# S5 in five steps per block beside ten gate columns, and six gate columns as three Strassen pairs

## The chip, the cores and the metric

The kernel runs on one core of a Trainium2 chip. The core has a matmul engine (PE), a vector engine (DVE), an activation engine (ACT), a general engine (POOL) and SP, whose queue issues most of the transfers between the chip's memory and the core's SBUF. Each engine works through its own list in order and waits for the others by semaphores. The metric is the device time of one execution in microseconds (us), the median of several.

## The reference, cut to what matters

A decoder layer on 1024 tokens of width 1024 in float32, with a state space branch (S5) and a recurrent branch (LRU) merged by sigmoid gates:

```python
h = rms_norm(x, g_pre)
proj = h @ w_in                       # 1024 x 5632
s5_x, s5_g, lru_x, lru_g, gate_s, gate_l = jnp.split(proj, IN_SPLITS, axis=-1)
y_s = s5_ssm(s5_x, ...)               # 32 groups of 16 channels, 64 complex states
glu_a, glu_b = jnp.split(jax.nn.gelu(y_s) @ w_glu, 2, axis=-1)
z_s = (glu_a * jax.nn.sigmoid(glu_b) * jax.nn.silu(s5_g)) @ w_bs
c = causal_depthwise_conv(lru_x, conv_w, conv_b)
z_l = (rg_lru(c, ...) * jax.nn.silu(lru_g)) @ w_bl
merged = jax.nn.sigmoid(gate_s) * z_s + jax.nn.sigmoid(gate_l) * z_l
x = x + rms_norm(merged @ w_out, g_post)
x = x + (p @ w_ple) * jax.nn.sigmoid(x @ w_ple_gate)
```

`w_in` has 44 columns of 128: 0 to 3 are s5_x, 4 to 7 s5_g, 8 to 27 the LRU's two inputs, 28 to 35 gate_s, 36 to 43 gate_l.

## The kernel before, in words

Every product is made to float32 accuracy from three passes: an operand is split into a high part, which ACT copies out in the reduced format fp32r, and a low part, the rest, which DVE subtracts (L234). `three` (L317, L319) issues high x high, high x low and low x high into one PSUM tile of 128 x 512; this is the wide matmul of the profile. Activations stand with features on partitions, so that a column of a weight matrix costs 8 blocks x 2 halves of the tokens x 3 = 48 wide matmuls.

`weight_plan` writes out the order of all weights: chunks of eight 128 x 128 blocks, loaded by SP into four buffers (`wraw`), and "quads" of four blocks, which become high and low in a ring of six (`wq`). `W.ahead` makes the next quads; a plain quad is used as it is. For some later matrices the kernel uses a Strassen scheme: quads named O2, S1, S3, S4 and A22 are sums of blocks (made on POOL, L194), and seven products stand for eight.

S5 runs in the background. `rows` multiplies one column and calls `tick` after every 12 wide matmuls; a tick advances each generator of the list `bg` to its next `yield`, so that the program's text sets the order on every engine, and S5's instructions fall between the wide matmuls. `s5_params` computes the parameters: DVE and ACT make sine and cosine (L608 to L613), POOL the powers `pw`, the factors `zr` and `zi` (L618 to L654) and the matrix `bb` (L681 to L683). Then DVE multiplies powers and factors into `pzt` (L669 to L675), PE transposes it (`pwT`, L691), and it goes to DRAM as `pt_d` and comes back as `wn`. `s5_ladders` builds the tables of rotations `etab` on DVE (L847 to L856).

For each of eight blocks `s5_main` has seven steps: `wn` is multiplied (L913, L915); py of the block before (8 matmuls, L983 and L984) with its gelu (L986) and four stores to `y_d` (L988), and the loads of the next block (`s5_load`); pkt (L928), which ACT copies to kt and SP writes into the block Toeplitz matrix `toep` in eight transfers (L934); pin (L939); ACT's copies pq (L946), DVE's rotation q, and POOL's weights `ca` for the next block (L902 to L904); four scans (L960) and the rotation back; q put together (L971, L972). py reads toep, ca and q; pin reads wn.

Under S5 lie the columns 36 to 43, 28 to 35, 4 and 5, in that order, each made by `light`: a column into a wide PSUM tile (`ps_L`), a sigmoid on ACT (L1015) into a tile `sg`, for columns 4 and 5 a product on DVE (L1017), and a store to DRAM (L1019). Then the pools of S5 are closed, and the LRU begins.

Of the kernel before, what the change touches and what calls it, by code (L numbers as in the profile page):

```python
# [31 lines left out]
SPAR = (("a_re", 48), ("a_im", 48), ("log_dt", 48), ("d_skip", 32), ("b", 1024), ("c", 1024))  # L32

F_ROWS = (0, 1, 4, 2, 5, 3, 6, 7)


def weight_plan():
    blocks, quads = [], []
# [75 lines left out]
    return blocks, quads  # L114


BLOCKS, QUADS = weight_plan()


FIRST = ("O2",)  # L120
# [15 lines left out]
class Weights:  # L136
# [42 lines left out]
    def sum(self, upto):  # L179
        G = self.nc.gpsimd  # L180
        while len(self.ready) <= min(upto, len(QUADS) - 1):
            i = len(self.ready)
            self.fetch(i)
            q = QUADS[i]
            s = self.sums
            if q[0] == "O2" and len(self.done) < i:
                return

            def add(name, a, b, op, into=None):
                if into is None:  # L190
                    s[name] = self.tmp.tile([P, HT], F32, tag=name, name=f"w{name}_{i}")
                else:
                    s[name] = s[into]
                G.tensor_tensor(s[name], s[a], s[b], op)  # L194

            if q[0] == "plain":
                _, c, o, n = q
# [7 lines left out]
                add("S1", "A21", "A22", ALU.add)  # L205
                add("S2", "S1", "A11", ALU.subtract)
            if q[0] in ("S4", "O4"):
                add("S4", "A12", "S2", ALU.subtract, "S2")
# [4 lines left out]
    def make(self, upto):  # L213
        nc = self.nc
        while len(self.done) <= min(upto, len(QUADS) - 1):
# [37 lines left out]
def tile_hybrid_trunk(  # L253
# [30 lines left out]
    u_d = dram.tile([NS, 8, 16, 8, P], F32, name="u_d")  # L284
    y_d = dram.tile([NS, 8, 8, 16, P], F32, name="y_d")
    pt_d = dram.tile([2, 8, 32 * P], F32, name="pt_d")

    def cst(shape, name, value=None, dt=F32):
        t = const.tile(shape, dt, name=name)
# [397 lines left out]
    def turn():  # L687
        pzt = turned[1]
        ps = px.tile([P, HT], F32, tag="px", name="pwT")
        for n in range(4):  # L690
# [3 lines left out]
        nc.sync.dma_start(pt_d.rearrange("r (h q) (g n) -> (q g) (r h) n", h=2, n=P),  # L694
                          pzs.rearrange("p (m n) -> p m n", n=P))

    prep = s5_params()
    def prep_all(n):
        for i, _ in enumerate(prep):
            if i % n == n - 1:  # L700
                yield

# [30 lines left out]
    def h_lo(k):  # L733
        for h in range(2):
            hi, lo = hplain(k, h)
            (G if h and k else V).tensor_tensor(lo, xt(k, HALF[h]), hi.bitcast(F32), ALU.subtract)  # L736

    def h_pages(names):
        for n, i0 in names:
# [94 lines left out]
    cosv = cosp[:, 32:].rearrange("p (m i) -> p m i", m=8)  # L834
    sinv = sinp[:, 32:].rearrange("p (m i) -> p m i", m=8)
    s5 = {}

    e_tab = {}

    def s5_ladders():  # L840
        t = page(6, "etab", F32)
        e1 = t[:, :512].rearrange("p (r i n) -> p r i n", r=2, i=16)
        e2 = t[:, 512:768].rearrange("p (r i n) -> p r i n", r=2, i=16)
        tm = t[:, 768:1024].rearrange("p (r i n) -> p r i n", r=2, i=16)
        e_tab[1], e_tab[2] = e1, e2
        for e, m0, steps in ((e1, 1, 4), (e2, 5, 3)):
            V.memset(e[:, 0, :, 0:1], 1.0)  # L847
            V.memset(e[:, 1, :, 0:1], 0.0)
            for m in range(steps):
                n = 1 << m  # L850
                er, ei = (v[:, m0 + m, :].unsqueeze(1).unsqueeze(3).to_broadcast([P, 2, 16, n]) for v in (cosv, sinv))
                src, dst, t_ = e[:, :, :, 0:n], e[:, :, :, n:2 * n], tm[:, :, :, :n]
                V.tensor_tensor(dst, src, er, ALU.mult)
                V.tensor_tensor(t_, src, ei, ALU.mult)
                V.tensor_tensor(dst[:, 0], dst[:, 0], t_[:, 1], ALU.subtract)
                V.tensor_tensor(dst[:, 1], dst[:, 1], t_[:, 0], ALU.add)  # L856
                if m % 2:
# [48 lines left out]
    def s5_main(hb, table, before):  # L906
# [11 lines left out]
            dd, ident[:16, :16].unsqueeze(1).to_broadcast([16, 4, 16]),  # L918
            d_skip[:, 4 * hb:4 * hb + 4].unsqueeze(2).to_broadcast([16, 4, 16]), ALU.mult)
        yield  # L920
        before()
        s5_load(hb + 1)
        yield

        kt = wk.tile([P, 576], F32, tag="kt", name=f"kt{hb}")[:16, :HT].rearrange("p (g m) -> p g m", g=4)
        ps = px.tile([P, HT], F32, tag="px", name=f"pkt{hb}")
        for g in range(4):
            T.matmul(ps[32 * g:32 * g + 16, :P], bb_1[:, 4 * hb + g, :],  # L928
                     ca[:, g, 0:8, :].rearrange("p d c -> p (d c)"), start=True, stop=True, tile_position=(0, 32 * g))
        for g in range(4):  # L930
            S.activation(kt[:, g, :], ps[32 * g:32 * g + 16, :P], AF.Copy)
        V.tensor_tensor(kt[:, :, 0:16], kt[:, :, 0:16], dd, ALU.add)
        for j in range(8):
            nc.sync.dma_start(toep[j::8, :, 16 * j:P], kt[:, :, 0:P - 16 * j])  # L934
        yield

        pin = px.tile([P, 2, 2, P], F32, tag="px", name=f"pin{hb}")
        for g in range(4):
            T.matmul(pin[:, g // 2, g % 2, :], win[:, g, :], U[:, g, :], start=True, stop=True)  # L939
        next(table, None)  # L940
        yield

# [47 lines left out]
        return finish  # L990

    def s5_all():
        for _ in prep:
            yield
        for _ in range(3):
            yield
        yield from s5_ladders()
        turned[0]()
        yield
        yield  # L1000
        turn()
        yield
        s5_load(0)
        yield from s5_table(0)
        s5_out_weights(0)
        before = lambda: None
        for hb in range(8):
            before = yield from s5_main(hb, s5_table(hb + 1) if hb < 7 else iter(()), before)
        yield
        before()  # L1010
# [11 lines left out]
    def ev_tile(name):  # L1022
        return ev.tile([P, NT], F32, tag="c", name=name)

    u3 = rows(hplain, "u3")
# [7 lines left out]
    bg.append(u_last())  # L1033
    bg.append(s5_all())
    for m in range(ND):
        light(36 + m, sgl_d[m], False, ev_tile)
    for m in range(ND):
        light(28 + m, sgs_d[m], False, ev_tile)
    for m in range(2):
        light(4 + m, sil_d[m], True, ev_tile)  # L1040
    drain()
    s5x.close()

    lctx = ExitStack()
    l1 = lctx.enter_context(tc.tile_pool(name="l1", bufs=1))
# [652 lines left out]
```

## Time and profile before

| | before |
|---|---|
| median of 3 runs | 928.75 us (928.25 to 928.76) |
| the profiled execution's own time | 928.25 us |
| its span | 926.5 us |
| PE busy | 919.0 us, 4228 matmul records |
| DVE, ACT, POOL busy | 624.6, 469.1, 150.6 us |
| moved by DMA | 134.21 MB |

The span runs from the first to the last instruction of the profiled execution; the execution's own time has a little around it. In a row of the timeline the first number is the start in us from the span's start, the second the duration (for a row with xN, of the N together), then engine, line, operation, output and inputs, shape, and in brackets how long the engine stood before it and what released it. Durations of matmuls overlap, so their spacing is read from the starts.

### The profile page before, as it was taken

Reading aid. Unit: us, or ns where it says so; the run is one execution under the profiler, and the core shown is the slowest. Engines: PE = TensorE matmul, PEld = TensorE weight load, DVE = VectorE, ACT = ScalarE, POOL = GpSimd, SP = SyncE. Lnnn points to the kernel's source line nnn. Section 1 sums busy time; section 2 is a strip of 40 time slices with the busy share of each in tenths; the row PEclk is TensorE's granted clock in tenths of the full one; section 3 lists DMA queues with packets and bytes.
Section 4 is the critical chain, followed back from the end, with each engine's and each line's share of the span. In section 5 each row is a group of like instructions: output and inputs, shape, how many; then the busy total and the mean of one; then the engine's idle time right before and its main releaser. Section 6 shows DMA issues by size and latency. Waiting matters only on the chain.

```text
span 926.5 us, 11716 instructions
## 1 busy us (share of the span) xinstructions
PE 919.0 (99%) x4228; PEld 760.3 (82%) x4228; DVE 624.6 (67%) x977; ACT 469.1 (51%) x714; POOL 150.6 (16%) x159
## 2 busy tenths in 40 slices
PE   9999999999999999999999999999999999999997
PEld 7888888888888888888888888888888887887886
DVE  6885566666664347766666767687862798886863
ACT  6643233444443356666666668544534355558531
POOL 1218112212220000000000000022322126422100
PEclk9999999999999999999999999999999999999999
DMA  9745445564533201111111116811479975499951
GB/s 358 277 126 160 126 142 166 172 171 133 173 97 113 74 29 52 52 46 51 52 52 52 47 34 216 291 56 55 141 255 244 247 193 206 119 245 233 301 184 56
DMA packets 70442, 134.21 MB, mean 145 GB/s; under 512 B 18416, under 2 KB 32880, under 8 KB 70384
## 3 DMA queue, kind: packets, MB, share of 16 engines
q1 hardware_dynamic: 64768, 122.72, 41.7%
q0 software_dynamic: 5472, 10.49, 6.3%
q8 instruction: 33, 0.54, 0.2%
q10 hardware_dynamic: 144, 0.26, 0.1%
q14 instruction: 25, 0.20, 0.1%
HBM read 95.30 MB, written 27.53 MB: 133 GB/s over the span
## 4 chain that ended last, share of the span: by engine, by line
PE 89%; issue 6%; DMA 2%; DVE 1%; POOL 1%; ACT 0%; POOLq 0%; SPq 0%
PE ps_L L319 16%; PE ps_L L317 8%; PE ps_rx L319 8%; PE ps_rg L319 8%; PE ps_rg L317 4%; PE ps_rx L317 4%; PE ps_F L319 3%; PE ps_u L319 3%; PE bZ L319 3%; PE ps_pg L319 2%; PE bW L319 2%; PE pg L319 2%; PE bX L319 2%; PE ps_ple L319 2%; PE ps_ea L319 2%
## 5 line engine op out<-in xcount | busy, mean ns | idle before, releaser
L319 PE MATMUL ps_L<-hB,wq 128*128 128x512 f32 x640 | 197.4, 390 | 0.0
L319 PEld LDWEIGHTS ps_L<-hB,wq 128*128 128x128 f32 x640 | 120.3, 188 | 24.3
L317 PE MATMUL ps_L<-hB,wq 128*128 128x512 f32 x320 | 127.1, 397 | 0.0
L222 ACT ACTIVATE wq<-wraw 128x512 fp32r<-128x512 f32 (+1 forms) x188 | 112.5, 613 | 24.1 <-issue 9.2
L234 DVE TENSOR_TENSOR wq<-wraw,wq 128x512 fp32r<-128x512 f32 (+1 forms) x152 | 105.0, 706 | 3.1 <-ACT wq L222 3.1
L319 PE MATMUL ps_rg<-hB,wq 128*128 128x512 f32 x320 | 98.5, 389 | 0.0
L319 PE MATMUL ps_rx<-hB,wq 128*128 128x512 f32 x320 | 98.5, 389 | 0.0
L319 PE MATMUL ps_pg<-x1hl,wq 128*128 128x512 f32 x240 | 74.9, 392 | 0.3 <-DVE x1hl L1374 0.2
L317 PEld LDWEIGHTS ps_L<-hB,wq 128*128 128x128 f32 x320 | 60.2, 188 | 13.3 <-issue 1.7
L319 PEld LDWEIGHTS ps_rg<-hB,wq 128*128 128x128 f32 x320 | 60.1, 188 | 12.5
L319 PEld LDWEIGHTS ps_rx<-hB,wq 128*128 128x128 f32 x320 | 60.1, 188 | 12.4
L194 POOL TENSOR_TENSOR wS<-wraw 128x512 f32<-128x512 f32 x8 | 12.4, 1549 | 354.8 <-DMA wraw<-w_blocks 343.3
L1078 DVE SCALAR_TENSOR_TENSOR c<-ps_rx,cp_t,c 128x1023 f32<-128x1023 f32 (+2 forms) x30 | 38.5, 1282 | 46.2 <-ACT c L1076 45.5
L317 PE MATMUL ps_rx<-hB,wq 128*128 128x512 f32 x160 | 62.3, 389 | 0.0
L317 PE MATMUL ps_rg<-hB,wq 128*128 128x512 f32 x160 | 62.3, 389 | 0.0
L319 PEld LDWEIGHTS ps_pg<-x1hl,wq 128*128 128x128 f32 x240 | 44.8, 188 | 11.5 <-DVE x1hl L1374 1.7
L1015 ACT ACTIVATE sg<-ps_L 128x1024 f32<-128x1024 f32 x20 | 20.5, 1027 | 59.7 <-issue 52.5
L226 POOL DMA_DIRECT2D wq<-wraw x36 | 31.8, 883 | 100.1 <-ACT wq L225 65.6
L317 PE MATMUL ps_pg<-x1hl,wq 128*128 128x512 f32 x120 | 47.0, 391 | 0.0
L319 PE MATMUL ps_u<-hB,wq 128*128 128x512 f32 x128 | 39.8, 392 | 0.4 <-DVE hB L736 0.4
L319 PE MATMUL ps_F<-ys,wq 128*128 128x512 f32 x128 | 39.4, 389 | 0.0
L1086 ACT ACT_TABLE_LOAD x9 | 11.5, 1283 | 51.2 <-DVE yr L1115 51.2
(360 smaller groups left out, 1927.0 us busy)
## 6 DMA issues: line engine op xcount, KB each, us to landing
wraw<-w_blocks SPq DMA_DIRECT2D x95, 512.0 KB
wq<-wraw POOLq DMA_DIRECT2D x36, 256.0 KB, 6.0
xt<-x_t SPq DMA_DIRECT2D x8, 512.0 KB
ple_d<-ple_sb SPq DMA_DIRECT2D x8, 512.0 KB
wn<-sbt SPq DMA_DIRECT2D x8, 512.0 KB
sgl_d<-sg SPq DMA_DIRECT2D x8, 512.0 KB
wn<-pt_d SPq DMA_DIRECT2D x16, 256.0 KB
sgs_d<-sg SPq DMA_DIRECT2D x8, 512.0 KB
```

What stands on the lines that cost most here:

```text
L194: G.tensor_tensor(s[name], s[a], s[b], op)
L222: nc.scalar.activation(hi, src, AF.Copy)
L226: nc.gpsimd.dma_start(lo.bitcast(F32), src, accum_op=ALU.add)
L234: self.nc.vector.tensor_tensor(lo, src, hi.bitcast(F32), ALU.subtract)
L317: T.matmul(ps, wh, xh, start=start, stop=False, skip_group_check=more)
L319: T.matmul(ps, a, b, start=False, stop=stop and a is (wh if xl_last else wl), skip_group_check=more)
L1015: S.activation(t, ps, AF.Sigmoid)
L1078: V.scalar_tensor_tensor(c[:, d:], ps[:, :NT - d], w_[3 - d], c[:, d:], ALU.mult, ALU.add)
L1086: S.activation(sq, ps, AF.Sigmoid)
```

## The change

The order of the weights: columns 4 and 5 come first under S5, then 36 to 43 as before; 28 and 29 stay plain, and 30 to 35 become three pairs. So ten gate columns, 12 with columns 4 and 5, lie beside S5, where 18 and a part of the next stage lay before.

```diff
+PAIRS = (30, 32, 34)
@@ weight_plan
-    for m in (*range(36, 44), *range(28, 36), 4, 5):
+    for m in (4, 5, *range(36, 44), *range(28, PAIRS[0])):
         plain(col("w_in", m, range(ND)))
+    first = [b for ks in (lo, hi) for m in PAIRS for b in col("w_in", m, ks)]
+    for o in range(0, len(first), 8):
+        light.add(chunk(first[o:o + 8]))
+        cut((len(blocks) - len(first[o:o + 8]), len(first[o:o + 8])))
+    for m in PAIRS:
+        c0, c1 = (chunk(col("w_in", m + i, range(ND))) for i in range(2))
+        light.add(c0)
+        quads.extend((part, c0, c1, 4) for part in ("O2", "S1", "S3", "S4", "A22"))
@@ Weights
-                G.tensor_tensor(s[name], s[a], s[b], op)
+                (self.nc.vector if light else G).tensor_tensor(s[name], s[a], s[b], op)
...
-            if q[0] == "plain" and BLOCKS[q[1][0]][0] in self.BY_DMA and i < len(QUADS) - 2 * ND:
+            if q[0] in ("plain", "A22") and (q[1] in LIGHT or BLOCKS[q[1][0]][0] in self.BY_DMA
+                                             and i < len(QUADS) - 2 * ND):
                 nc.scalar.activation(lo, src, AF.Copy, scale=-1.0)
                 nc.gpsimd.dma_start(lo.bitcast(F32), src, accum_op=ALU.add)
```

The light quads' sums are made on DVE, and the lows of the six plain ones and of A22 by ACT and an accumulating transfer of POOL's queue.

S5 starts before the column u3 instead of after it, its ladders run as a generator of their own, and a block has five steps:

```diff
@@ h_lo
+        nc.sync.dma_start(h_d[k], xt(k))
@@ s5_main
         yield
         before()
         s5_load(hb + 1)
-        yield
+        if hb == 7:
+            h_load(2, "T2", "B22")
...
+        pin = px.tile([P, 2, 2, P], F32, tag="px", name=f"pin{hb}")
+        for g in range(4):
+            T.matmul(pin[:, g // 2, g % 2, :], win[:, g, :], U[:, g, :], start=True, stop=True)
         for g in range(4):
             S.activation(kt[:, g, :], ps[32 * g:32 * g + 16, :P], AF.Copy)
...
-        yield
-
-        pin = px.tile([P, 2, 2, P], F32, tag="px", name=f"pin{hb}")
-        for g in range(4):
-            T.matmul(pin[:, g // 2, g % 2, :], win[:, g, :], U[:, g, :], start=True, stop=True)
+        if hb == 7:
+            h_load(6, "T4", "B21")
@@ s5_all
-        for _ in prep:
-            yield
-        for _ in range(3):
-            yield
-        yield from s5_ladders()
+        for at in prep:
+            if at == "trig":
+                bg.append(s5_ladders())
+            yield
...
         for hb in range(8):
+            if hb == 6:
+                bg.append(t_early())
+            if hb in (2, 5):
+                yield
             before = yield from s5_main(hb, s5_table(hb + 1) if hb < 7 else iter(()), before)
@@
+    bg.append(s5_all())
     u3 = rows(hplain, "u3")
...
-    bg.append(s5_all())
+    for m in range(2):
+        light(4 + m, sil_d[m], True, ev_tile)
```

The normalised input h is stored to DRAM (`h_d`, eight stores of 512 KB) and its quarters B11, B12, B21, B22 are read back into free pages (`h_load`, 16 reads of 256 KB); DVE makes of them the operands T1 to T4 of the scheme (`t_early`, `t_build`). After S5 the pools are closed, four pages and single PSUM banks take their place, and the pairs run:

```diff
+    s5x.close()
+    gp = gctx.enter_context(tc.tile_pool(name="gp", bufs=1))
+    page_pool.update({i: gp for i in (14, 15, 16, 17)})
...
+    wide_ctx.close()
+    gps = gctx.enter_context(tc.tile_pool(name="gps", bufs=1, space=PSUM))
+    bg.append(t_build())
+    for p_ in range(3):
+        tick()
+        lprod(xs[p_], hq["B11"], True)
+        S.activation(lu[:, p_], xs[p_], AF.Copy)
+        tick()
+    for p_, m in enumerate(PAIRS):
+        lprod(xs[p_], hq["B21"], False)
+        gate_out(m, 0, o, xs[p_])
...
+    for p_, m in enumerate(PAIRS):
+        lprod(z, lop["T2"], True)
+        V.tensor_tensor(z, z, u, ALU.add)
...
+        lprod(w_, lop["T1"], True)
...
+        lprod(z, lop["T3"], False)
+        lprod(w_, hq["B22"], False)
+        lprod(z, lop["T4"], False)
...
+    pw2 = wide_ctx.enter_context(tc.tile_pool(name="pw2", bufs=3, space=PSUM))
```

`lprod` is 12 wide matmuls, `gate_out` a sigmoid and its store. PE has 36 wide matmuls fewer in all.

The first place is PE around the transposition `pwT`. Before, it stands in the third column under S5 (`ps_L` is a gate column, `hB` the parts of h, `wq` the quads):

```order
L319 MATMUL ps_L_985<-hB_376,wq_821 128x512
L319 MATMUL ps_L_985<-hB_375,wq_821 128x512
L691 MATMUL pwT<-ident,pzt 128x128 x4
L317 MATMUL ps_L_985<-hB_373,wq_821 128x512
L319 MATMUL ps_L_985<-hB_374,wq_821 128x512
```

In the changed kernel the rows at the same place read (the lines of `three` are L329 and L331 there):

```order
L329 MATMUL ps_u_716<-hB_446,wq_545 128x512
L331 MATMUL ps_u_716<-hB_447,wq_545 128x512
L331 MATMUL ps_u_716<-hB_446,wq_545 128x512
L703 MATMUL pwT<-ident,pzt 128x128 x4
L329 MATMUL ps_L_876<-hB_374,wq_549 128x512
L331 MATMUL ps_L_876<-hB_375,wq_549 128x512
```

pwT has moved from row 401 of PE's list to row 293, between the column u3 (`ps_u`) and the first column under S5. On DVE, what stands ahead of it there, from the cosine on:

```order
L625 TENSOR_SCALAR cosp<-scratch 128x160
L656 RECIPROCAL scratch<-scratch 128x32
L681 TENSOR_TENSOR pzt<-pw,scratch 128x256
L683 TENSOR_TENSOR pzt<-pzt 128x256
L684 TENSOR_TENSOR pzt<-pw,scratch 128x256
L686 TENSOR_TENSOR pzt<-pzt 128x256
L687 TENSOR_TENSOR pzt<-pzt,sgn 128x256
L720 MEMSET etab 128x16
L726 TENSOR_TENSOR etab<-etab,cosp 128x32
```

Before, the ladders (`etab`) came ahead of `pzt`; now they come behind it.

The second place is a block's work on PE. Before, 12 wide matmuls stand between py and pkt, and 12 between pkt and pin:

```order
L983 MATMUL py_1471<-U_1112,toep 128x128
L984 MATMUL py_1471<-q_1379,ca_1200 128x128
L317 MATMUL ps_L_1494<-hB_373,wq_1269 128x512
L319 MATMUL ps_L_1494<-hB_375,wq_1269 128x512
L928 MATMUL pkt_1513<-ca_1384,bb 16x128 x4
L317 MATMUL ps_L_1494<-hB_373,wq_1269 128x512
L319 MATMUL ps_L_1494<-hB_375,wq_1269 128x512
L939 MATMUL pin_1543<-U_1305,wn_1301 128x128 x4
L317 MATMUL ps_L_1494<-hB_441,wq_1338 128x512
```

In the changed kernel:

```order
L999 MATMUL py_1155<-U_903,toep 128x128
L1000 MATMUL py_1155<-q_1062,ca_985 128x128
L944 MATMUL pkt_1176<-ca_1067,bb 16x128 x4
L948 MATMUL pin_1181<-U_1012,wn_1008 128x128 x4
L329 MATMUL ps_L_1096<-hB_444,wq_928 128x512
```

py, pkt and pin now stand together, and 60 wide matmuls lie between pin and the next py (72 after the second and the fifth pin).

The third place is the end of S5. On SP, ahead of the last block's toep (`fT` are the quarters of h, `wraw` the weights, `y_d` the output of block 6, `kt` the last pkt):

```order
L1041 DMA sgl_d<-sg_2087 128x1024
L172 DMA wraw_2137<-w_blocks 128x1024
L1087 DMA fT_2168<-h_d 128x512 x3
L172 DMA wraw_2139<-w_blocks 128x1024
L1087 DMA fT_2197<-h_d 128x512 x3
L1004 DMA y_d<-ysb_2153 8x16x128 x4
L953 DMA toep<-kt_2173 16x512
L953 DMA toep<-kt_2173 16x4x112
```

Before, a gate's store, one weight load and the four stores to `y_d` stood there. On ACT, behind the last block's py:

```order
L1002 ACT_TABLE_LOAD
L1002 ACTIVATE ysb_2309<-py_2310 128x512
L1037 ACT_TABLE_LOAD
L1037 ACTIVATE sg_2324<-ps_L_2227 128x1024
L232 ACTIVATE wq_2346<-wraw_1952 128x512
L236 ACTIVATE wq_2346<-wraw_1952 128x512
L1144 ACTIVATE lu<-lX_2338 128x512
```

The gelu (`ysb`) stands ahead of the sigmoid (`sg`) of the last plain column, and the first copy of a pair's product (`lu`, from the bank `lX`) behind both.

More of the change, by code (lines that the diff above doesn't have):

```diff
@@ L34 @@
 F_ROWS = (0, 1, 4, 2, 5, 3, 6, 7)
+PAIRS = (30, 32, 34)
 def weight_plan():
-    blocks, quads = [], []
+    blocks, quads, light = [], [], set()
     def chunk(names):
@@ L113, in weight_plan @@
             cut(c)
-    return blocks, quads
-BLOCKS, QUADS = weight_plan()
+    return blocks, quads, light
+BLOCKS, QUADS, LIGHT = weight_plan()
 FIRST = ("O2",)
@@ L185, in sum @@
             s = self.sums
+            light = q[1] in LIGHT
             if q[0] == "O2" and len(self.done) < i:
@@ L207, in sum @@
             if q[0] in ("S4", "O4"):
-                add("S4", "A12", "S2", ALU.subtract, "S2")
+                add("S4", "A12", "S2", ALU.subtract, "A12" if light else "S2")
             if q[0] == "S3":
@@ L286, in tile_hybrid_trunk @@
     pt_d = dram.tile([2, 8, 32 * P], F32, name="pt_d")
+    h_d = dram.tile([ND, P, NT], F32, name="h_d")
     def cst(shape, name, value=None, dt=F32):
@@ L695, in turn, with s5_ladders @@
                           pzs.rearrange("p (m n) -> p m n", n=P))
+    cosv = cosp[:, 32:].rearrange("p (m i) -> p m i", m=8)
+    sinv = sinp[:, 32:].rearrange("p (m i) -> p m i", m=8)
+    e_tab = {}
+    def s5_ladders():
+        t = page(6, "etab", F32)
+        e1 = t[:, :512].rearrange("p (r i n) -> p r i n", r=2, i=16)
+        e2 = t[:, 512:768].rearrange("p (r i n) -> p r i n", r=2, i=16)
+        tm = t[:, 768:1024].rearrange("p (r i n) -> p r i n", r=2, i=16)
+        e_tab[1], e_tab[2] = e1, e2
+        for e, m0, steps in ((e1, 1, 4), (e2, 5, 3)):
+            V.memset(e[:, 0, :, 0:1], 1.0)
+            V.memset(e[:, 1, :, 0:1], 0.0)
+            for m in range(steps):
+                n = 1 << m
+                er, ei = (v[:, m0 + m, :].unsqueeze(1).unsqueeze(3).to_broadcast([P, 2, 16, n]) for v in (cosv, sinv))
+                src, dst, t_ = e[:, :, :, 0:n], e[:, :, :, n:2 * n], tm[:, :, :, :n]
+                V.tensor_tensor(dst, src, er, ALU.mult)
+                V.tensor_tensor(t_, src, ei, ALU.mult)
+                V.tensor_tensor(dst[:, 0], dst[:, 0], t_[:, 1], ALU.subtract)
+                V.tensor_tensor(dst[:, 1], dst[:, 1], t_[:, 0], ALU.add)
+                if m % 2 and m0 == 1:
+                    yield
     prep = s5_params()
     def prep_all(n):
-        for i, _ in enumerate(prep):
+        for i, at in enumerate(prep):
+            if at == "trig":
+                bg.append(s5_ladders())
             if i % n == n - 1:
@@ L833, in tile_hybrid_trunk @@
     c_1, c_2 = (g32(cc[:, i]) for i in range(2))
-    cosv = cosp[:, 32:].rearrange("p (m i) -> p m i", m=8)
-    sinv = sinp[:, 32:].rearrange("p (m i) -> p m i", m=8)
     s5 = {}
[L838 to L857, printed above, removed]
-                    yield
     def s5_table(hb):
@@ L1031, in u_last, with lpage, t_low, t_high @@
         yield
-    bg.append(u_last())
+    lf = {}
+    lop = {"T2": [3, 14], "T1": [9, 16], "T3": [17, 2], "T4": [7, 8]}
+    def lpage(n, i):
+        lop[n][i] = quarter(page(lop[n][i], f"l{n}{i}"))
+    def t_low(n):
+        for k in range(4):
+            V.tensor_tensor(lop[n][1][:, k, :], lf[n][:, k], lop[n][0][:, k, :].bitcast(F32), ALU.subtract)
+    def t_high(n):
+        lpage(n, 0)
+        for k in range(4):
+            S.activation(lop[n][0][:, k, :], lf[n][:, k], AF.Copy)
+    def t_subs(n, a, b):
+        for k in range(4):
+            V.tensor_tensor(lf[n][:, k], lf[a][:, k], lf[b][:, k], ALU.subtract)
+            if k % 2:
+                yield
@@ L1034, in tile_hybrid_trunk, with t_early, h_load @@
+    def t_early():
+        yield from t_subs("T1", "T1", "T3")
+        while "T2" not in lf:
+            yield
+        yield
+        yield
+        yield from t_subs("T2", "T2", "T1")
+        t_high("T2")
+        t_high("T1")
+    def h_load(i, t, n):
+        lf[t] = quarter(page(i, f"f{t}", F32))
+        for k in range(4):
+            nc.sync.dma_start(lf[t][:, k], h_d[4 * (n[1] == "2") + k][:, HALF[n[2] == "2"]])
     bg.append(s5_all())
+    u3 = rows(hplain, "u3")
+    bg.insert(0, u_last())
@@ L1035, in tile_hybrid_trunk, with t_build @@
+    for m in range(2):
+        light(4 + m, sil_d[m], True, ev_tile)
     for m in range(ND):
         light(36 + m, sgl_d[m], False, ev_tile)
-    for m in range(ND):
+    for m in range(PAIRS[0] - 28):
         light(28 + m, sgs_d[m], False, ev_tile)
-    for m in range(2):
-        light(4 + m, sil_d[m], True, ev_tile)
     drain()
     s5x.close()
+    gctx = ExitStack()
+    gp = gctx.enter_context(tc.tile_pool(name="gp", bufs=1))
+    page_pool.update({i: gp for i in (14, 15, 16, 17)})
+    def t_build():
+        lpage("T2", 1)
+        t_low("T2")
+        yield
+        lpage("T1", 1)
+        t_low("T1")
+        yield
+        yield from t_subs("T3", "T2", "T3")
+        t_high("T3")
+        yield from t_subs("T4", "T4", "T2")
+        lpage("T3", 1)
+        lpage("T4", 0)
+        for k in range(4):
+            S.activation(lop["T4"][0][:, k, :], lf["T4"][:, k], AF.Copy)
+        t_low("T3")
+        yield
+        lpage("T4", 1)
+        t_low("T4")
@@ new lines, in lprod, with gate_out, gbank @@
+    def lprod(ps, op, start):
+        W.ahead()
+        for k, wb in enumerate(W.next()):
+            three(ps, wb, (op[0][:, k, :], op[1][:, k, :]), start and k == 0, k == 3, not start)
+    def gate_out(m, h, t, src):
+        S.activation(t, src, AF.Sigmoid)
+        nc.sync.dma_start(sgs_d[m - 28][:, HALF[h]], t)
+    wide_ctx.close()
+    gps = gctx.enter_context(tc.tile_pool(name="gps", bufs=1, space=PSUM))
+    def gbank(i, name):
+        return gps.tile([P, HT], F32, tag=f"gb{i}", name=name)
@@ L1044, in tile_hybrid_trunk @@
+    drain()
+    gctx.close()
+    pw2 = wide_ctx.enter_context(tc.tile_pool(name="pw2", bufs=3, space=PSUM))
     lctx = ExitStack()
```

25 lines of the change are left out of this document (24 added, 1 removed).

## The prediction

> **What bounds the kernel now.** I read the page's busy table first, then its chain, then PE's waits.
>
> ```profile
> PE 919.0 (99%) x4228; PEld 760.3 (82%) x4228; DVE 624.6 (67%) x977; ACT 469.1 (51%) x714; POOL 150.6 (16%) x159
> ...
> PE 89%; issue 6%; DMA 2%; DVE 1%; POOL 1%; ACT 0%; POOLq 0%; SPq 0%
> ```
>
> PE (the matmul engine) is busy for 919.0 of 926.5 us and carries 89% of the chain. Its waits (engine, tile, releaser: total, times, longest) say the same:
>
> ```profile
> PE warm L500 <- DVE halfpi L291: 1.1, 1, 1.1
> PE ps_ple L317 <- DVE p_hi L526: 0.8, 1, 0.8
> PE ps_u L319 <- DVE hB L736: 0.4, 1, 0.4
> ```
>
> These are the three longest, two of them at the start. So a matmul taken away is worth its full time, and any wait put on PE costs its full time: there is no slack to hide it in. What a wide matmul costs is read from the column u3, 48 of them between these two starts:
>
> ```profile
> 67.12 0.39 PE L317 MATMUL ps_u<-hB,wq 128*128 128x512 f32 x1
> ...
> 78.00 0.39 PE L317 MATMUL ps_L<-hB,wq 128*128 128x512 f32 x1
> ```
>
> 10.88/48 = 0.2267 us each.
>
> **What is saved.** PE issues 36 wide matmuls fewer (each pair of columns as 7 products of 12, not 8): 36 x 0.2267 = 8.2 us. The S5 matmuls stay, but pkt and pin now stand directly behind py:
>
> ```profile
> 226.35 0.38 PE L983 MATMUL py<-U,toep 128*128 128x128 f32 x2
> ...
> 228.05 0.48 PE L317 MATMUL ps_L<-hB,wq 128*128 128x512 f32 x1
> ...
> 230.96 0.41 PE L928 MATMUL pkt<-ca,bb 128*16 128x128 f32 x8
> 231.31 0.50 PE L317 MATMUL ps_L<-hB,wq 128*128 128x512 f32 x1
> ...
> 234.16 1.05 PE L939 MATMUL pin<-U,wn 128*128 128x128 f32 x8
> 234.97 0.48 PE L317 MATMUL ps_L<-hB,wq 128*128 128x512 f32 x1
> ```
>
> py takes 1.70, pkt 0.35, pin 0.81 us. Joining them can save between nothing and 8 x 0.35 = 2.8 us; I take 0.5, since nothing here shows a cost of turning from one kind to the other.
>
> **First wait: pwT.** It moves from PE's row 401 to row 293, straight behind u3, where PE arrives at 78.00. Its input pzt hangs on a chain that is not moved:
>
> ```profile
> 69.35 1.28 ACT L608 ACT_TABLE_LOAD   x1
> ...
> 72.25 0.25 POOL L618 TENSOR_TENSOR pw<-scratch,cosp 128x32 f32<-128x32 f32 x1 [20.90 <-DVE cosp L613]
> ...
> 83.83 0.25 POOL L654 TENSOR_TENSOR scratch<-scratch 128x32 f32<-128x32 f32 x1
> 84.38 1.09 POOL L681 TENSOR_TENSOR bb<-braw,scratch 128x512 f32<-128x512 f32 x1
> ...
> 98.24 0.42 DVE L669 TENSOR_TENSOR pzt<-pw,scratch 128x256 f32<-128x256 f32 x1
> ...
> 100.61 0.43 DVE L675 TENSOR_TENSOR pzt<-pzt,sgn 128x256 f32<-128x256 f32 x1
> 102.49 0.60 PE L691 MATMUL pwT<-ident,pzt 128*128 128x128 f32 x4
> 102.84 0.47 PE L317 MATMUL ps_L<-hB,wq 128*128 128x512 f32 x1
> ```
>
> The sine's table load stands behind the copies of the third u column on ACT in both kernels, so POOL's powers run from 72.25 to 84.08 as before. Seven DVE operations of pzt use the powers; the first can start before POOL ends, the other six (2.5 us, by the rows of 98.24 to 101.04) can not, so pzt is there at 86.6 at best. It is later if they collide with POOL's bb, as the ladders do now:
>
> ```profile
> 83.06 0.07 DVE L847 MEMSET etab<- 128x16 f32 x1
> ...
> 86.05 1.14 DVE L853 TENSOR_TENSOR etab<-etab,cosp 128x128 f32<-128x128 f32 x1
> ...
> 97.44 0.28 DVE L853 TENSOR_TENSOR etab<-etab,cosp 128x128 f32<-128x128 f32 x1
> ```
>
> The same form takes 1.14 beside POOL and 0.28 without it. All six at 1.14 from 84.1 end at 90.9; I take 88.5. PE therefore waits 8.6 to 12.9 us at pwT. More follows: the ladders (15.2 us from 83.06 to pzt) now come behind pzt on DVE and end near 101 (88.5 + 12.5, since POOL's work runs out near 96), then two lows (1.2), six table operations of 0.35, column 4's product with its sigmoid (1.22) and
>
> ```profile
> 247.89 1.22 DVE L913 TENSOR_TENSOR wn<-wn 128x1024 f32<-128x1024 f32 x1
> 249.15 0.69 DVE L915 TENSOR_TENSOR wn<-wn 128x512 f32<-128x512 f32 x1
> ```
>
> make the first wn ready near 107. Without a wait the first pin would be reached at 78.00 + 0.35 + 72 x 0.2267 + 0.35 = 95.0. So PE's delay at this pin, the wait at pwT within it, is **12 us** (8.6 if the ladders hide; 16 if pzt comes at 90.9 and PE also runs slow behind its wait). Matmuls behind a standstill are slow in this trace:
>
> ```profile
> 7.46 0.63 PE L317 MATMUL ps_ple<-p_hi,wq 128*128 128x512 f32 x1
> ...
> 10.42 0.40 PE L319 MATMUL ps_ple<-p_hi,wq 128*128 128x512 f32 x1
> ```
>
> Seven intervals of 0.42. The Trainium skill, "TensorE: Matmul & The Clock Gate", Part 1, has a rule for it: an idle window of about 3.4 us halves the array's clock, and about 3.4 us of work restore it. By it some 8 matmuls after pwT would take 0.2 us more each, an estimate of 1.6 us; no run here shows a standstill in the middle yet. This would fall ahead of the pin, which waits for DVE anyway, and would not change the sum.
>
> **Second: the rhythm of S5.** Between one pin's end and the next lie 60 matmuls, py and pkt (72 at two places, for the extra steps): 60 x 0.2267 + 1.70 + 0.35 = 15.65 us. Before, the next wn was ready 14.9 us after a pin's end (234.97 to 249.84), so the margin is 0.8 us. DVE has to do it in less time:
>
> ```profile
> 150.00:175.00 25.00, 25.00 (x130) 20.72 (x129) 17.69 (x36) 9.85 (x18) 5.26 (x5) 1.00 0.53 161
> ```
>
> (stretch; busy of PE, PEld, DVE, ACT, POOL; clock, DMA share, GB/s.) DVE worked 0.71 of a period of 22.3 us (84 matmuls and 3.2 us), 15.8 us; two lows of 0.6 drop out, 14.6 remain in a period of 16.5. That is 88%, with collisions that lengthen whatever meets POOL. I put 0.7 us on each of the four plain transitions (0 to 1.5) and none on the two with extra steps. The last is worse, because toep's eight transfers for block 7 now stand on SP behind reads of h and a weight load:
>
> ```profile
> wq<-wraw POOLq DMA_DIRECT2D x36, 256.0 KB, 6.0
> ```
>
> (the accumulating transfers, us from issue to landing) and SP's timeline:
>
> ```profile
> 231.45 2.59 SPq L988 DMA_DIRECT2D y_d<-ysb  x4
> 234.14 5.11 SPq L934 DMA_DIRECT2D toep<-kt  x8
> ```
>
> That load (wraw_2139) reuses a buffer which the accumulating DMAs read, landing some 7.5 us after py6 ends; then three reads, y_d 2.6 and toep 5.1 and its landing make 18.7, where py7 comes at 60 x 0.2267 + 0.35 + 0.81 = 14.8. I count 3.7 (0 to 7). Together **6.5 us** (0 to 13).
>
> The eight stores of h (4 MB) go into the stretch
>
> ```profile
> 25.00:50.00 25.00, 24.63 (x122) 20.22 (x122) 22.75 (x44) 17.25 (x30) 9.21 (x7) 1.00 0.67 238
> ```
>
> whose DMA is idle a third of the time, and weights are loaded ahead: nothing, or 3 us if weights come late.
>
> **Third: the way into the pairs.** S5's pools and the wide PSUM pool close first. lX may start only when ACT has released the last wide tile, and ACT has the gelu of block 7 ahead of it:
>
> ```profile
> 295.33 1.28 ACT L986 ACT_TABLE_LOAD   x1 [5.67 <-issue]
> 296.62 0.60 ACT L986 ACTIVATE ysb<-py 128x512 f32<-128x512 f32 x1
> ...
> 302.08 1.03 ACT L1015 ACTIVATE sg<-ps_L 128x1024 f32<-128x1024 f32 x1
> ```
>
> Table, gelu, table, sigmoid: 1.28 + 0.60 + 1.28 + 1.03 plus handing over, 4.5 us, with PE standing. DVE's lows in S5's memory must also wait until the y_d stores and the last gate's store have landed, some 8 us after py7:
>
> ```profile
> 297.25 2.57 SPq L988 DMA_DIRECT2D y_d<-ysb  x4
> ...
> 304.28 1.29 DVE L234 TENSOR_TENSOR wq<-wraw,wq 128x512 fp32r<-128x512 f32 x2
> ```
>
> From there 30 DVE operations of 0.6 us (the pairs' light sums among them, which POOL would have made before) stand up to the low of lW's weights: 8.2 + 18.2 = 26.4, while PE asks for it at 4.5 + 84 x 0.2267 = 23.5, and the next product's operands end about 1.5 later still. I take **8.5 us** (4.5 to 10.5). Opening the wide pool again waits for the last sigmoid: 0.9 (0 to 1).
>
> **Sum.** 926.5 - 8.2 - 0.5 + 12 + 6.5 + 8.5 + 0.9 = 945.7 us of span. The profiled execution took 928.25 for a span of 926.5, 1.75 more, and the median of the runs lies 0.5 above it: **947 us**. Every wait at its lower bound and the whole 2.8 saved gives 926.5 - 8.2 - 2.8 + 8.6 + 4.5 = 928.6, + 1.75, some 930; every one at its upper gives 926.5 - 8.2 + 16 + 13 + 10.5 + 1 + 3 = 961.8 + 1.75, some 963.
>
> **Rivals.** (a) The rhythm holds, and DVE has its ladders ready under the column after pwT: 926.5 - 8.7 + 8.6 + 0.5 + 8 + 0.9 = 935.8, 938 us. For it: 0.8 us of margin, and lows can slip behind. Against: 88% of DVE. (b) The transfers become the bound: the 150 to 175 row has the DMA engines 0.53 busy, times 22.3/16.5 = 0.72, with the reads of h on top; if toep is then late by 2 us in seven blocks, 947 + 14 = 961. Against: 0.72 is not full. (c) The other side: both standstills hide, because PE takes ready wide matmuls ahead of the waiting pwT and lX; then only the saving counts: 926.5 - 8.7 + 1.75, about 920 us. It decides for faster from the point at which all added waits together stay under 8.7 - 1.9 = 6.8 us. Against it (PE's timeline):
>
> ```profile
> 38.66 0.73 PE L319 MATMUL ps_u<-hB,wq 128*128 128x512 f32 x2 [0.37 <-DVE hB L736]
> 39.23 0.39 PE L317 MATMUL ps_u<-hB,wq 128*128 128x512 f32 x1
> ```
>
> PE stood for 0.37 us ahead of an L319, which reads the low part of h, and started the L317 behind it, which reads the high part that ACT makes first, only afterwards. The Trainium skill, "TensorE: Matmul & The Clock Gate", Part 2, states that matmuls stay in program order and that only weight loads are pulled ahead; the row agrees, and by that rule (c) could not happen.
>
> **Chances.** The forecast 0.68, (a) 0.20, (b) 0.08, (c) 0.04. The range 937 to 958 takes in (a) and most of the upper bounds. A measurement of this kernel tells changes above 0.2% (1.9 us) from none: slower 0.92, within 0.2% of it 0.04 (all lower bounds at once), faster 0.04.
>
> **What would show it.** Right: a wait of PE at pwT on DVE pzt of 8.6 to 12.9 us; a second at the first pin on wn; a third at lX on ACT's sigmoid near 4.5 us and at lW or lZ on lows; waits under 1.5 us at pins two to seven. Wrong: pwT's wait under 5 us, which would mean that POOL's powers start earlier; no wait at lX; or waits at py on toep in every block, which is (b).

## The result and the profile after

The changed kernel took 953.57 us (median of 4 runs, 952.65 to 954.77) beside 928.50 us for the kernel before on the same chip: 1.0271 times the time, 95% interval 1.0253 to 1.0289. It is slower, by 25 us. The forecast was 947, the range 937 to 958.

The page's busy table of the changed kernel (span 952.4 us; the profiled execution took 954.15 us):

```profile
PE 917.3 (96%) x4192; PEld 757.3 (80%) x4192; DVE 658.4 (69%) x1030; ACT 493.0 (52%) x763; POOL 155.0 (16%) x168
...
PE 58%; issue 7%; DVE 6%; DMA 4%; POOL 1%; ACT 1%; SPq 0%; POOLq 0%; DVEq 0%; ACTq 0%
```

The 36 matmuls are gone from PE (4228 to 4192 records). The shares of the chain that ended last can't be set beside those of before: here they add up to 77% only, because the chain as printed reaches back no further than 200.95 us. PE's waits name the places (engine, tile, line, releaser: total, times, longest):

```profile
PE pin L948 <- ACT ysb L1002: 10.4, 7, 1.7
PE pwT L703 <- DVE pzt L683: 6.2, 1, 6.2
PE lX L329 <- ACT sg L1037: 4.3, 1, 4.3
PE pwT L703 <- DVE etab L721: 4.3, 1, 4.3
PE lZ L329 <- ACT lu L1159: 1.2, 1, 1.2
...
PE ps_rx L329 <- ACT lc L1129: 0.7, 1, 0.7
```

Before, the three longest were 1.1, 0.8 and 0.4 us. Nearly all of the loss lies ahead of the first matmul of the LRU, `ps_rx`. It stood here before and stands there now:

```profile
300.55 0.39 PE L317 MATMUL ps_rx<-hB,wq 128*128 128x512 f32 x1
```

```profile
325.87 0.50 PE L329 MATMUL ps_rx<-hB,wq 128*128 128x512 f32 x1 [0.69 <-ACT lc L1129]
```

That is 25.3 us later; from there to the end it is 626.0 us before and 626.5 now. The wait at pwT comes in two pieces, because pzt's four blocks are transposed one by one, and what follows it runs slowly:

```profile
84.12 0.69 PE L703 MATMUL pwT<-ident,pzt 128*128 128x128 f32 x2 [6.19 <-DVE pzt L683]
89.09 0.69 PE L703 MATMUL pwT<-ident,pzt 128*128 128x128 f32 x2 [4.28 <-DVE etab L721]
89.43 0.78 PE L329 MATMUL ps_L<-hB,wq 128*128 128x512 f32 x1
...
94.62 0.40 PE L329 MATMUL ps_L<-hB,wq 128*128 128x512 f32 x1
```

(The second wait is put down to the first row of the ladders; the last operation of pzt, which it really needs, ran directly ahead of that, from 87.89 to 89.03.) Twelve wide matmuls lie between 89.43 and 94.62: 5.19 us where 12 x 0.2267 = 2.72 would do. The same happens behind the wait at lX. Two rows of the stretches (busy of PE, PEld, DVE, ACT, POOL; clock; DMA share; GB/s) show it in the granted clock:

```profile
84.00:95.00 11.00, 6.60 (x18) 5.06 (x19) 10.80 (x16) 4.71 (x6) 10.05 (x9) 0.52 0.45 133
...
143.00:201.00 58.00, 52.98 (x287) 44.28 (x287) 42.19 (x80) 25.27 (x45) 13.62 (x12) 1.00 0.57 162
```

So the account of the waits up to `ps_rx` is: 8.2 saved; 10.5 at pwT and 2.5 for slow matmuls behind it; 10.4 at the seven later pins; 4.3 at lX and 2.3 behind it (12 matmuls from 263.85 to 268.88 in 5.03 us); 1.2 at lZ, 0.7 at ps_rx. That sums to +23.7 of the 25.3. The waits are counted from the end of the matmul before, as the profile models it; read from start to start against the spacings of the kernel before, the same places give 11.1 at pwT and 2.4 behind it, 10.9 at the pins, 4.4 at lX and 2.3 behind it, 1.7 at lZ and 0.8 at ps_rx. With 8.2 saved, and 0.1 saved by joining py, pkt and pin, that is all of the 25.3 us.

The prediction had small waits at the pins, from DVE's load; what causes these was in no step of it. Six of the seven are 1.67 us long. This is one of them, on PE:

```profile
145.17 0.41 PE L944 MATMUL pkt<-ca,bb 128*16 128x128 f32 x8
147.25 0.49 PE L948 MATMUL pin<-U,wn 128*128 128x128 f32 x2 [1.67 <-ACT ysb L1002]
```

ACT in the same stretch:

```profile
145.31 1.28 ACT L1002 ACT_TABLE_LOAD   x1 [2.99 <-issue]
146.60 0.60 ACT L1002 ACTIVATE ysb<-py 128x512 f32<-128x512 f32 x1
```

py, pkt and pin take turns in the PSUM pool `px`, which has two banks. py has one and pkt the other, so pin must wait until the gelu has read py, and the gelu stands behind a table load: 1.28 + 0.60 behind py, 1.67 of it in PE's way.

### The profile page after: what moved, and what is told of

The parts are those of the page before. It is cut to its first block, busy times and chain, and to the rows that moved or that the text cites. A ratio compares the mean times of both kernels' runs of the same rounds, so it can differ in the third digit from the quotient of the medians.

```text
span 952.4 us, 11842 instructions
## 1 busy us (share of the span) xinstructions
PE 917.3 (96%) x4192; PEld 757.3 (80%) x4192; DVE 658.4 (69%) x1030; ACT 493.0 (52%) x763; POOL 155.0 (16%) x168
## 4 chain that ended last, share of the span: by engine, by line
PE 58%; issue 7%; DVE 6%; DMA 4%; POOL 1%; ACT 1%; SPq 0%; POOLq 0%; DVEq 0%; ACTq 0%
PE ps_rx L331 8%; PE ps_rg L331 8%; PE ps_rx L329 4%; PE ps_rg L329 4%; PE bZ L331 3%; PE ps_pg L331 2%; PE ps_L L331 2%; PE bW L331 2%; PE bX L331 2%; PE pg L331 2%; PE ps_F L331 2%; PE lZ L331 2%; PE ps_ea L331 2%; PE ps_eb L331 2%; PE bZ L329 1%
## 5 line engine op out<-in xcount | busy, mean ns | idle before, releaser
L331 PE MATMUL ps_L<-hB,wq 128*128 128x512 f32 x448 | 139.7, 393 | 0.0
L232 ACT ACTIVATE wq<-wraw 128x512 fp32r<-128x512 f32 (+1 forms) x191 | 114.5, 613 | 28.0 <-DMA wraw<-w_blocks 10.5
L245 DVE TENSOR_TENSOR wq<-wraw,wq 128x512 fp32r<-128x512 f32 (+1 forms) x146 | 101.4, 709 | 15.0 <-ACT wq L232 14.9
L331 PEld LDWEIGHTS ps_L<-hB,wq 128*128 128x128 f32 x448 | 85.3, 190 | 17.7
L331 PE MATMUL ps_rx<-hB,wq 128*128 128x512 f32 x320 | 98.5, 389 | 0.0
L331 PE MATMUL ps_rg<-hB,wq 128*128 128x512 f32 x320 | 98.5, 389 | 0.0
L329 PE MATMUL ps_L<-hB,wq 128*128 128x512 f32 x224 | 89.0, 397 | 0.0
L331 PE MATMUL ps_pg<-x1hl,wq 128*128 128x512 f32 x240 | 74.5, 391 | 0.7 <-DVE x1hl L1507 0.5
L331 PEld LDWEIGHTS ps_rg<-hB,wq 128*128 128x128 f32 x320 | 60.1, 188 | 12.5
L331 PEld LDWEIGHTS ps_rx<-hB,wq 128*128 128x128 f32 x320 | 60.1, 188 | 12.5
L237 POOL DMA_DIRECT2D wq<-wraw x45 | 39.6, 881 | 169.6 <-ACT wq L236 129.7
L329 PE MATMUL ps_rx<-hB,wq 128*128 128x512 f32 x160 | 62.4, 390 | 0.7 <-ACT lc L1129 0.7
L329 PE MATMUL ps_rg<-hB,wq 128*128 128x512 f32 x160 | 62.2, 389 | 0.0
L331 PEld LDWEIGHTS ps_pg<-x1hl,wq 128*128 128x128 f32 x240 | 44.7, 188 | 11.3 <-DVE x1hl L1507 2.0
L329 PEld LDWEIGHTS ps_L<-hB,wq 128*128 128x128 f32 x224 | 42.8, 191 | 8.7
L329 PE MATMUL ps_pg<-x1hl,wq 128*128 128x512 f32 x120 | 46.9, 391 | 0.0
L331 PE MATMUL ps_u<-hB,wq 128*128 128x512 f32 x128 | 39.8, 392 | 0.4 <-DVE hB L774 0.4
L331 PE MATMUL ps_F<-ys,wq 128*128 128x512 f32 x128 | 39.4, 389 | 0.0
L329 PEld LDWEIGHTS ps_rx<-hB,wq 128*128 128x128 f32 x160 | 30.0, 188 | 7.3 <-ACT lc L1129 1.1
```

What stands on the lines that cost most here:

```text
L245: self.nc.vector.tensor_tensor(lo, src, hi.bitcast(F32), ALU.subtract)
L329: T.matmul(ps, wh, xh, start=start, stop=False, skip_group_check=more)
L331: T.matmul(ps, a, b, start=False, stop=stop and a is (wh if xl_last else wl), skip_group_check=more)
```

## The experiments

All times are medians; the kernel before took between 928.08 and 928.47 us beside them. First three edits that undo one suspected wait each, and the three together.

**py one step earlier**, so that 12 wide matmuls cover the gelu:

```diff
+        before()                    # py of the block before
         yield
-        before()
         s5_load(hb + 1)
```

> One edit: py of the block before is issued one step earlier, 12 wide matmuls ahead of pkt and pin. py, pkt and pin take turns in a PSUM pool of two banks, so in the changed kernel pin must wait until the gelu has read py. Theory PSUM: the seven waits at pin (10.4 us together) go, nothing takes their place, 943 us (942 to 945). Rival DVE: the block is bound by its DVE chain and its transfers as the prediction had it, the wait moves to py (on q or toep) or to pin (on wn), and the time stays above 949 us.

Measured 950.94 us, 2.6 less than the change. From PE's waits of this run:

```profile
PE py L1000 <- DVE q L988: 5.7, 8, 1.7
```

The waits at pin on the gelu are gone, which shows that they came from the order on the two banks. But DVE's q is not ready one step earlier, and PE stands at py instead. So both readings hold: the banks made the wait, and DVE's chain stood close behind it.

**The parameters of S5 ahead of the loop over the u columns** (the ladders still behind pzt, pwT at the same row of PE):

```diff
     bg.append(prep_all(7))
+    for _ in range(6):
+        tick()
...
         turned[0]()
+        bg.append(s5_ladders())
+        yield
```

> One edit: the parameters of S5 (sine, powers, pzt) are issued ahead of the loop over the u columns, so that POOL's powers start some 12 us earlier; pwT and everything behind it stand on PE where they stood. Theory: the wait at pwT (10.5 us) and the slow matmuls behind it (2.5 us) go, 940.6 us (939 to 942). Rival: the ladders, tables and wn then decide, the first pin waits for wn by 5 us or more, 945 us or above.

Measured 948.91 us, 4.7 less: the rival's direction. POOL's powers start at 66.89, only some 5 us earlier than before, because the sine waits for some 14 us of small DVE operations (51.26 to 65.25), and pzt still meets POOL's bb. Of PE's waits are left:

```profile
PE pin L948 <- ACT ysb L1002: 10.0, 6, 1.7
...
PE pwT L703 <- DVE etab L721: 3.8, 1, 3.8
...
PE pin L948 <- DVE wn L930: 0.8, 1, 0.8
```

At pwT 4.2 us remain of 10.5. The first pin moved from 108.66 to 103.13 and now waits for wn, though by 0.8 us and not by 5: behind pwT stands the chain of ladders, tables and wn, as the prediction had it.

**The last plain column's sigmoid ahead of the gelu of block 7:**

```diff
-            S.activation(ysb..., ps, AF.Gelu_apprx_tanh)   # and its four stores
+            late.append(out) if hb == 7 else out()
 ...
         light(28 + m, sgs_d[m], False, ev_tile)
     drain()
+    late[0]()
```

> One edit: the sigmoid of the last plain column stands ahead of the gelu of block 7 on ACT. Theory chain: the wait at lX (4.35 us) and the slow matmuls behind it (2.3 us) go, but DVE's chain of lows starts with the landing of the last stores as before, so PE waits as long at lZ and lW instead: 952.5 to 954 us. Rival: the wait at lX counts by itself, 946.9 us.

Measured 953.36 us: the chain. lX starts at once, and the wait appears, not yet at lZ or lW, but ahead of the sixth product into the lX banks, behind a copy on ACT that stands behind high parts which wait for DVE:

```profile
277.12 0.80 PE L329 MATMUL lX<-hB,wq 128*128 128x512 f32 x1 [3.99 <-ACT lu L1152]
```

and on DVE, in the same run:

```profile
266.76 4.90 DVE L1068 TENSOR_TENSOR lT<-fT,lT 128x512 fp32r<-128x512 f32 x8 [12.39 <-DMA y_d<-ysb]
```

DVE's first low in the memory of S5 starts at 266.76 here and at 267.21 in the changed kernel, when the last stores of S5 have landed. That decides the way into the pairs, not ACT's order.

**The three together:**

> The three edits together. If the first two add up and the third gives nothing, 953.6 - 10.4 - 13.0 = 930.2 us (928.5 to 931.5); if the third also counts by itself, 923.5 us; if DVE or the transfers become the bound once the waits are gone, 935 us or above.

Measured 948.43 us, hardly less than the second alone: the last of the three expectations. Each wait had another behind it: pwT 3.8, lX 4.0, py on q 3.2 and on toep 2.2, pin on DVE's kt 1.9.

**The S5 half alone**, columns 30 to 35 plain, no pairs, no h in DRAM:

```diff
-PAIRS = (30, 32, 34)
+PAIRS = ()
...
-        nc.sync.dma_start(h_d[k], xt(k))
...
```

> The S5 half of the change alone: S5 in five steps beside the same twelve columns, then columns 30 to 35 plain; no pairs, no store and no reading back of h. PE has the matmuls of the kernel before. Theory: the waits at pwT (10.5 us, and 2.5 us of slow matmuls behind it) and at the pins (10.4) are this half's, 928.3 + 23.4 = 951.7 us (950 to 953.5), and the pairs give back about what they cost (8.2 us saved; 4.35 + 2.3 + 1.6 + 1 lost). Rival: part of the waits comes from the stores and reads of h on SP's queue, 945 us or below.

Measured 951.67 us, as the sum of the two waits gave it (951.7). PE's waits are the same ones, 10.4 at pin and 5.9 + 4.3 at pwT. So nearly all of the loss is the five-step S5 and its early start, the traffic of h has no visible part in it, and the pairs lose again all of the 8.2 us of matmuls that they save: with them the kernel takes 953.57 - 951.67 = 1.9 us more, or 1.5 when each is taken against the kernel before beside it, a difference that the intervals (1.0253 to 1.0289 and 1.0238 to 1.0269) don't separate.

**Two pairs, and two plain columns behind S5**, under which its memory comes free:

```diff
-PAIRS = (30, 32, 34)
+PAIRS = (32, 34)
 ...
     s5x.close()
+    bg.append(t_build())
+    for m in range(2, 4):
+        light(28 + m, sgs_d[m], False, lambda name: gp.tile(...))
     wide_ctx.close()
```

> Only columns 32 to 35 as two pairs; columns 30 and 31 are plain and run after S5's pools are closed, so that the stores land and DVE makes the pairs' operands under them. PE has 12 wide matmuls more than the changed kernel (2.7 us). Theory: all of the standstill between S5 and the pairs comes from the memory that S5 gives back late; it goes (4.35 + 2.3 slow matmuls + 1.6), about 1 us at the new lX stays: 953.6 + 2.7 - 8.2 + 1 = 949.1 us (948 to 950). Rival: the pairs' own operands on DVE are the bound wherever they stand, the waits stay, 956 us.

Measured 948.35 us. The wait at lX fell from 4.3 to 1.1 us and the one at lZ is gone, although PE has 12 matmuls more. This shows that the standstill comes from the pairs standing directly behind S5. It doesn't separate the memory that S5 gives back late (DVE's first low in it starts at 266.42 here, hardly earlier than 267.21) from the making of the operands behind it: the two plain columns cover both.

**pwT four steps later**, as the run before with one plain column behind S5:

```diff
         turned[0]()
         yield
         yield
+        yield
+        yield
+        yield
+        yield
         turn()
```

> As the run two_pairs_tail, but pwT and all of S5 behind it come four steps (one column, 10.9 us) later, while pzt and the ladders are issued where they were; one plain column stays behind S5. Theory: the wait at pwT and the slow matmuls behind it go (13 us), the first pin then waits some 1.8 us for wn: 948.35 - 13 + 1.8 = 937 us (935 to 939). Rival: the first pin is held by SP's queue or DVE's ladders and takes most of it back, 943 us or above.

Measured 947.37 us, 1.0 less and within the noise of the two: the rival. PE does not wait at pwT, but (PE's waits of this run)

```profile
PE pin L948 <- ACT ysb L1002: 10.4, 7, 1.7
PE ps_L L331 <- DVE wq L245: 5.5, 1, 5.5
PE pin L948 <- ACT kt L950: 1.7, 1, 1.7
```

the low parts of the weights now stand behind pzt and the ladders on DVE (the low that PE waited for ran at 95.02), and on SP the store of pt_d stood until 101.29 behind a weight load that SP issued only at 100.85. So pwT's row alone does not make the 13 us: a wait of the same kind appears at the lows, behind the same work of DVE. The reading that fits is that DVE and POOL have the set-up of S5 to do in one go while PE has one column to run.

**pin ahead of py**, pkt one step earlier, and POOL's work tile in the memory of pq; then the same **with pq ahead of the gelu** on ACT (the added order in outline):

```diff
+        kt = ...; pkt; kt copies
         yield
+        pin
+        pq copies                   # second run only
         before()                    # py, gelu, stores
```

> Two edits that belong together: pkt is issued one step earlier and pin ahead of py, so that pin takes its bank from a tile that ACT read long before; and POOL's work tile for ca shares memory with pq instead of kt, so that ca no longer waits for toep's transfers. Theory banks (the order on the two PSUM banks made the wait, and DVE's chain from pin to the next wn, 14.4 us in the changed kernel, fits into the 15.7 us between pins once pin leads): the waits at pin go and none follows, 943 to 945.5 us. Rival DVE (DVE's load in the shorter period is the bound whatever the order): PE waits on wn or q instead, 949 us or above, like the run with py one step earlier.

> As the run pin_first, with one edit more: ACT copies pin (pq) right behind the kt copies and ahead of the gelu of py. In pin_first the gelu with its two table loads stood between pin and pq on ACT, which delayed DVE's chain by 3.8 us per block. Theory order on ACT: the chain from pin to the next wn then takes about 14.8 us of the 15.7 us between pins, PE waits at no pin, 943 to 946 us. Rival DVE: 949 us or above.

Measured 962.26 and 947.24 us. In the first, pin no longer waits for the gelu, but pq, and with it DVE's chain, does: pin ends at 146.0, and pq starts at 149.85 behind (ACT's timeline)

```profile
148.06 1.28 ACT L1002 ACT_TABLE_LOAD   x1 [2.94 <-issue]
149.36 0.60 ACT L1002 ACTIVATE ysb<-py 128x512 f32<-128x512 f32 x1
149.85 1.54 ACT L962 ACTIVATE pq<-pin 64x256 f32<-64x256 f32 x4
```

PE's waits at the pins are 11.1 us there with no releaser named ("issue") and 1.3 on kt. The times point to what was awaited: each of the four without a releaser starts 0.10 us after the end of DVE's work on wn (here on PE and on DVE):

```profile
164.78 1.13 PE L947 MATMUL pin<-U,wn 128*128 128x128 f32 x8 [2.60 <-issue]
```

```profile
163.99 0.69 DVE L930 TENSOR_TENSOR wn<-wn 128x512 f32<-128x512 f32 x1
```

In the second, PE's waits in the rhythm are

```profile
PE py L999 <- DMA toep<-kt: 2.2, 1, 2.2
PE pin L947 <- DVE kt L942: 1.3, 1, 1.3
...
PE pin L947 <- ACT wq L236: 0.6, 1, 0.6
...
PE pin L947 <- issue: 0.3, 2, 0.2
```

4.4 us instead of 10.4, and the time is 6.3 us less. The waits put down to ACT's wq and to "issue" also end some 0.1 us behind wn. What remains of the rhythm is thus what the prediction had named: DVE and, at the last block, toep. Between the two expectations, the result lies nearer to the order on ACT.

**Together with two pairs.** In the first of the following two runs S5 starts four steps later and pin stands ahead of py, without the edit of pq; the second spends the four steps on early parameters, two steps of delay and two extra steps in blocks:

> Two pairs; S5 starts four steps (one column) later, so that pwT comes 10.9 us later on PE; one plain column after S5; pin ahead of py as in the run pin_first. If the three causes (pwT too early, the banks, the memory of S5) are all and add up: 953.6 + 2.7 - 13.0 - 10.4 - 8.2 + 1 = 925.7 us, a little faster than before (924.5 to 928). If pins wait for wn or q once the other waits are gone: 932 us or above.

> As the run two_pairs_late, but the four steps are spent otherwise: the parameters of S5 are issued early, S5 starts two steps later, and two more blocks get an extra step. If DVE's chain between pins is what remains, the two extra steps show as less waiting at pins than in two_pairs_late, by 1 to 3 us; if nothing remains there, both are equal within 1 us, 925.7 us (924.5 to 928).

Measured 956.09 and 950.39 us. Both carry the fault of pin_first (waits at pin of 11.1 and 13.6 us, without a releaser, all ending 0.10 us behind wn), so they don't settle whether the three causes add up. In the second, 6.0 of the 13.6 us are at the first pin, where DVE stood 4.6 us for the landing of wn. The other 7.6 against 11.1 us show the two extra steps as less waiting, by 3.5 us, which is the side of the expectation on which DVE's chain between pins remains. In the first, the delay stood ahead of pzt too, and pwT still waited 9.3 + 0.9 us. The second with pq ahead of the gelu, the store of pt_d on ACT's queue, and h read later:

> As the run two_pairs_prep, with pq ahead of the gelu, the store of pt_d on ACT's queue instead of SP's (where it stood behind a weight load that waited 9 us for its buffer) and the reads of h behind the first blocks. If the three causes (pwT too early, the order of pin, pq and gelu, the memory of S5) are all that the change lost: 928.5 - 5.4 (24 matmuls) + 1.2 (lX) + 1 to 3 = 925 to 928 us. If DVE or the queue still decide, 932 us or above.

Measured 934.78 us (933.01 to 937.77), 1.0072 times the kernel before (1.0048 to 1.0097): the second expectation. The wait at the first pin fell from 6.0 to 1.4 us. No version tried beats the kernel before. Its largest waits:

```profile
PE pin L947 <- DVE kt L942: 2.9, 1, 2.9
PE pin L947 <- issue: 1.6, 2, 1.4
PE lX L329 <- ACT sg L1041: 1.2, 1, 1.2
```

It has 12 wide matmuls more than the change and is 18.8 us faster. With 24 fewer than the kernel before (5.4 us) it still loses some 12 us; the waits at the pins, 4.5, are the largest part. It stays open whether the rest could be hidden too.

## Why the prediction was right, and where not

The direction, and that the loss is waits of a PE without slack, came out as forecast. Point by point, in the order of the sum:

- **Saved, 8.2:** right; 36 records fewer. Of the 0.5 for joining py, pkt and pin, 0.1 was seen: from start to start the joined group takes 3.1 us without its wait where the three took 2.85, but before, twelve wide matmuls took 2.91 behind py and 2.86 behind pkt instead of 2.72, a cost of turning that the prediction did not see, and most of that is gone.
- **First wait, 12:** the wait at pwT was taken as 10.5 and is 10.5; wn was expected near 107 and was multiplied at 107.73. The delay at the first pin is 108.66 - 95.0 = 13.7. The surplus is the step that said the slow matmuls would change nothing, since the pin waits for DVE anyway: PE, slowed by 2.5 us, came to the pin at 108.66, 0.9 us after wn was done, and the wait on wn that the prediction gave as a sign did not come. The sum was near because two bounds lay close together; the run with early parameters, where pin waits for wn, shows DVE's chain as the next one.
- **Rhythm of S5, 6.5:** this step failed in its mechanism. It weighed DVE's load and toep's transfers and did not ask what pin waits for in PSUM: two banks for three groups that now stand together. Measured are 10.9 us from start to start (10.4 in the table of waits), 4.4 more, and the pins waited 1.67 us where less than 1.5 was the sign of being right. The step's own bound is real but second: 5.7 us at q when py comes earlier, 4.4 us at kt, toep and wn when the order is mended. That the total still lay within the range is in part luck: the 6.5 was the price of another cause.
- **Way into the pairs, 8.5 and 0.9:** right in place and in its bound. The wait at lX was worked out as 4.5 and is 4.3; that DVE's 30 operations behind the landing of the last stores set the end was shown by the run with the sigmoid first. The pieces differ: slow matmuls behind lX, 2.3 us that the step left out, stand where a wait on lows at lW was expected, and the wait at lZ is on ACT's copy `lu`, which waits for DVE. From start to start they are 4.4 + 2.3 + 1.7 = 8.4, and 0.8 at ps_rx.
- **Rivals:** (a) was wrong in the rhythm. (b) did not happen: the wait on toep shows at one block and only once other waits are gone. (c) did not happen; every wait listed shows PE standing at the instruction that is next in its order.

The sum was 6.7 us of span short (945.7 against 952.4). From start to start these are 4.4 at the later pins, 1.4 at pwT and behind it, 0.4 for the joining and 0.6 behind ps_rx, less 0.1 at the pairs.

## What to carry to other kernels

Before matmul groups that share a small PSUM pool are moved together, follow the pool's turns: the next owner of a bank waits for the last reader of the one before, with whatever that reader has ahead of it on its engine, here a table load. Where the bound engine has no slack, undoing one wait tells little; price the one behind it too (here 10.4 us of waits were worth 2.6 or 6.3, according to the edit). And a saving that needs memory from the stage before should stand a column or two behind that stage, not directly after it.

## What the runs showed of the hardware

A long standstill of PE costs more than its length. In the changed kernel, after waits of 4.28 us (with 6.19 just ahead) and 4.35 us, the next twelve 128x512 matmuls started 0.43 and 0.42 us apart on average instead of 0.227, 2.5 and 2.3 us lost, with a granted clock of 0.52 in the stretch around pwT. The pins' waits of 1.67 us, three of them in the stretch from 143 to 201, left it at 1.00. The Trainium skill, "TensorE: Matmul & The Clock Gate", Part 1, says that an idle window of about 3.4 us halves the clock until about as long a busy one; the changed kernel's trace agrees on both sides of that length, and the estimate that the prediction drew from it (1.6 us) was low against the 2.5 measured, since the slow stretch lasted 5.2 us.

Neither figure is fixed across the runs. In the run with pq ahead of the gelu the same waits at pwT (6.00 and 4.29 us) were followed by twelve matmuls in 4.25 us, 1.5 lost. And in the run with pin ahead of py alone (pin_first) a wait of 2.56 us, on PE,

```profile
223.65 1.32 PE L947 MATMUL pin<-U,wn 128*128 128x128 f32 x8 [2.56 <-issue]
```

was followed by a granted clock of 0.53 (226 to 228) and a py of 3.2 us instead of 1.7, while the waits of 2.60 and 2.35 us ahead of it in that run left py at 1.7. So the length of a single wait does not decide it between these lengths; what else does, no run here shows.
